# Transposes of the queries and of the pool layers' first mixed group one strip later, inverses behind the second queries, blocks for the solve collected by column: a four-layer decoder trunk on one core

## The chip, the core and the metric

The kernel runs on one core of a Trainium2 chip. The metric is the device time of one execution in microseconds (us), the median of several runs; less is better.

The core's engines work side by side, each through its own queue in order: TensorE (PE in the profile, with its weight loads as PEld) does the matmuls and transposes, VectorE (DVE), ScalarE (ACT) and GpSimd (POOL) the elementwise work, and SyncE (SP) issues the weight transfers. An instruction waits at the head of its queue until the semaphores it needs are set, and everything behind it on that engine waits too.

## What is computed

The reference is a trunk of four residual layers over 256 tokens of width 1024, and a final normalization:

```
for i in range(DEPTH):                       # 4
    kind, j = i % N_MIXERS, i // N_MIXERS    # 0 pool, 1 GDN, 2 MLA
    h = rmsnorm(x, norm_g[i])
    y = mixer[kind](h, ...)
    x = x + y
return rmsnorm(x, final_g)

def pool_mixer(h, w_in, w_grp, scale, w_out):
    u, gate = split(h @ w_in)                # 2 x 2048 columns
    p = windowed causal means of u, minus u  # 4 groups of 512 channels
    p = einsum('bsgi,gio->bsgo', p, w_grp)
    return (p * scale * silu(gate)) @ w_out

def gdn_mixer(h, w_in, conv_w, ...):         # 8 heads, chunks of tokens
    q, k, v, gate, b, a = split(h @ w_in)
    q, k, v = silu(causal_depthwise_conv(q, k, v))
    A = I + strict_lower(beta k k^T * decay)
    u, w = solve(A, [beta v, beta k exp(g)]) # triangular solve
    ...                                      # recurrence over the chunks
    return (rmsnorm(o) * silu(gate)) @ w_out
```

Layers 0 and 3 are pool layers, layer 1 is the GDN (gated delta rule) layer, layer 2 is MLA attention.

## The kernel before

**Strips.** All products with weights go through `project`, one strip of 512 weight columns at a time. SyncE loads 512 KB of weights; ScalarE rounds them (`whi`, a cast, L149 or L153), VectorE or, for a few, GpSimd takes the rest (`wlo`, L150 or L154); TensorE then multiplies three times for each product, at L162. In the channel form (`chan`) a strip has 96 matmuls of 128x256 and puts channels on the partitions. In the row form it has 48 matmuls of 128x512 and puts tokens on the partitions. Products go to banks of PSUM, transposes to others (`tp`), small matmuls to `aux`.

**Who sets the order.** A scheduler orders the instructions of every engine. `later(ins, ...)` binds what is written inside it behind the instructions named. The kernel keeps such marks in `mark`: `strip` is the last matmul of the last channel strip, `conv` the last step of the last convolution on VectorE, `dve` the last `wlo` there, `back` the last copy of the blocks on GpSimd.

**GDN layer.** Its steps stand in a list: `g` gate strips (row form), `k` and `q` strips of keys and queries in two halves, `v` values, `V` and `c` the last values in two parts, `d` decays, `a` the lower triangles, `s` the substitution, `b` the blocks back, `i` the inverses, `n` the query norms, `u` the first chunk's news. A half of keys or queries is one channel strip, a convolution over its four tiles (first tap on ScalarE at L768, three more on VectorE at L771), a silu on ScalarE (L813), and eight 128x128 transposes into `tp` (L819), whose squares are summed (L822, L823). `against` multiplies keys with queries or keys (L832). The solve: lower triangles LT (L841) are copied in blocks of 32x32 into Lg (ScalarE L864, GpSimd L866), transposed on VectorE (L869) and solved row by row on GpSimd (L875, L879). `blocks_back` transposes the result (L885) and copies it into T, two copies on ScalarE (L892) and two on GpSimd (L894). `inverses` transposes T on VectorE (L961) and joins the blocks with matmuls (L970, L976, L984, L988, L994).

**Pool layers.** For each group of 512 channels, in the order 3, 2, 1, 0, there is a gate strip, a strip of the inputs, the window sums, and one step behind it `mixed`, the product with the group's weights. The first group has the row form: its result y (L587) is turned by eight transposes (L593) before it can go into the output product. In `mixed` of that group they are written directly behind L587, between other strips.

**The head.** `Normed.rest` makes each layer's normalized input in pieces `h` (L399, L404) from two buffers, and `Final` writes them to the output with a transfer for each.

Of the kernel before, what the change touches and what calls it, by code (L numbers as in the profile page):

```python
# [42 lines left out]
def trunk(ctx: ExitStack, tc: tile.TileContext, x, positions, norm_g, pool_w_in, pool_w_grp,  # L43
# [130 lines left out]
    def project(src, ks, act, cols=CW, chan=False, tail=0, done=None, cuts=1,  # L174
# [29 lines left out]
        banks = [[bank(acc, "acc") for _ in range(cuts)] for _ in range(NT)]  # L204

        def rows(t, c, k0, n, parts):
            o, sl = banks[t][c][:, :width], slice(c * width, (c + 1) * width)
            for x, y in ((0, 0), (0, 1), (1, 0)) if n == 1 else ((0, None), (1, 0)):
                for j in range(n):
                    k = k0 + j  # L210
                    for z in (0, 1) if y is None else (y,):
                        mm(o, act(k, t * P, P)[x], parts[j][z][:, sl],
                           k == first and x == z == 0, k == last and x == 1, block or width)

        held = []
        for u, (k0, n) in enumerate(ks):
            held.append((k0, n, ready.pop(0) if ready else unit(k0, n)))
            if u < len(ks) - tail:
                now, held = held, []
            elif u == len(ks) - 1:  # L220
                now = held
            else:
                continue
            for t in range(NT):
                for c in range(cuts):
                    for one in now:
                        rows(t, c, *one)
                    if done and u == len(ks) - 1:
                        done(t, c, banks[t][c][:, :width])
        return [b[0] for b in banks]  # L230
# [146 lines left out]
    class Normed:  # L377
# [5 lines left out]

        def begin(self, t, a):
            sl = slice(a, a + CUT)
            self.early[t, a] = wh.tile([P, CUT], F32, tag="hg", name="hg")
            nc.gpsimd.tensor_tensor(out=self.early[t, a], in0=xs[t][:, sl], in1=self.g[:, sl],  # L387
                                    op=ALU.mult)

        def rest(self, t):  # L390
# [4 lines left out]
            for a in range(0, D, CW):  # L395
                h = wh.tile([P, CW], F32, tag="h", name="h")
                cut = CUT if (t, a) in self.early else 0
                sl = slice(a + cut, a + CW)
                nc.vector.scalar_tensor_tensor(out=h[:, cut:], in0=xs[t][:, sl], scalar=r[:, 0:1],  # L399
                                               in1=self.g[:, sl], op0=ALU.mult, op1=ALU.mult)  # L400
                hs.append(h)
                if not cut:
                    continue
                mark["rest"] = nc.scalar.activation(h[:, :CUT], self.early.pop((t, a)), AF.Copy,  # L404
                                                    scale=r[:, 0:1]).ins
# [29 lines left out]
    class Final(Normed):  # L435
        def __init__(self):
            super().__init__(final_g.rearrange("(a d) -> a d", a=1))

# [75 lines left out]
    def pool_layer(i, j, hT):  # L514
# [59 lines left out]
        def mixed(g, pT, gs):  # L574
# [13 lines left out]
            for a in range(2):  # L588
                ps = bank(tps, "tp")
                for b in range(2):  # L590
                    for t in range(NT):
                        c = 2 * a + b
                        nc.tensor.transpose(ps[:, b * S + t * P:b * S + (t + 1) * P],  # L593
                                            y[t][:, c * P:(c + 1) * P], ident)
                split_out((ps.rearrange("p (c s) -> p c s", c=2),
                           yT.many(g * 4 + 2 * a, 2, 0, S), None))

        waiting, loaded = None, []
        for g in order:
            gs = gate(g)  # L600
            if lead:
# [8 lines left out]
            if waiting:  # L610
                mixed(*waiting)
# [58 lines left out]
    def gdn_layer(i, j, hT):  # L670
# [23 lines left out]
        order = "g0 k0 d a0 k1 a1 s q0 g1 v0 v1 v2 b q1 i n V3 c3 g2 u0 u1 g3".split()  # L694
# [93 lines left out]
        Lg = LX[:, :M * B].rearrange("p (m c) -> p m c", m=M)  # L788
# [11 lines left out]
        def channels(dst, c0, hf, which):  # L800
# [4 lines left out]
            for b in range(2):  # L805
# [3 lines left out]
                for c in range(2):  # L809
# [3 lines left out]
                    mark["silu"] = nc.scalar.activation(o, v, AF.Silu).ins  # L813
            for c in range(0, 4, 2):
# [32 lines left out]
        def keys(hf):  # L847
            hs = slice(4 * hf, 4 * hf + 4)
            channels(kT, GDN_QK, hf, 0)
            n, r = ssq[:, 0, :, hs], s2[:, :, hs]  # L850
# [5 lines left out]
        def lower(hf):  # L856
            for t in range(NT):
                against(LT, kT, s2, hf, t)
                hs = slice(4 * hf, 4 * hf + 4)
                for d in range(Q):  # L860
                    dd = slice(d * B, (d + 1) * B)
                    o = Lg[dd, t * H + 4 * hf:t * H + 4 * hf + 4]
                    if t:
                        nc.scalar.copy(o, LT[t][dd, hs, dd])  # L864
                    else:
                        nc.gpsimd.tensor_copy(o, LT[t][dd, hs, dd])  # L866

        def substitution():
            nc.vector.transpose(Lb, Lg.rearrange("p m c -> p c m")[:, :, None, :].to_broadcast(  # L869
                [P, B, 2, M]))  # L870
# [12 lines left out]
        def blocks_back():  # L883
# [4 lines left out]
            for d in range(Q):  # L888
                dd = slice(d * B, (d + 1) * B)
                o = Ts[dd, :, :, dd].rearrange("p t h c -> p (t h) c")  # L890
                if d % 2:
                    nc.scalar.copy(o, tv[dd])  # L892
                else:
                    mark["back"] = nc.gpsimd.tensor_copy(o, tv[dd]).ins  # L894
# [3 lines left out]
        def queries(hf):  # L898
            if hf == 0:
                at_.extend(big("attnT", H, P) for _ in range(NT))  # L900
            channels(qT, 0, hf, 1)
# [101 lines left out]
        def news(hf):  # L1003
# [3 lines left out]
            for b in range(2):  # L1007
# [6 lines left out]
                for c in range(2):  # L1014
# [5 lines left out]
                 "c": values_done}  # L1020
        once = {"s": substitution, "d": decays, "b": blocks_back, "i": inverses,
                "n": query_norms}
        for name in order:
            if name in "bi":

                with later(mark["strip"], mark["dve" if name == "i" else "conv"]):
                    once[name]()
            elif name in once:
# [418 lines left out]
```

## Time and profile before

| | |
|---|---|
| runs | 809.26, 811.97, 812.18 us; median 811.97 |
| the profiled execution | 814.1 us, of it 812.4 us from first to last instruction |
| mean granted clock of TensorE | 0.994 |
| strips v0 to g3 of the GDN layer | about 230 to 320 us of the span |
| last pool layer's first mixed group | about 700 to 712 us |

Busy time is the time in which an engine executes. A window lists it for a stretch of the span, with the clock that TensorE was granted (1.00 is full speed). A timeline row is: start, length, engine, line, operation, result and operands, shapes, count, and in brackets the idle time just before it and what ended it. A row of the waits says who waited for whom: us in total, times, longest. Matmuls overlap, so that a row's length is longer than the distance to the next.

### The profile page before, as it was taken

The numbers are of one execution on the slowest core, as the hardware profiler recorded it, in microseconds if no ns is written. First come the engines' busy times: TensorE is split into PE (matmuls) and PEld (weight loads), VectorE is DVE, ScalarE is ACT, GpSimd is POOL, SyncE is SP. The second block draws the span as 40 slices with busy tenths as digits, with TensorE's granted clock in tenths as the row PEclk, the third lists the DMA queues.
The fourth block names the chain that finished last, engine by engine and source line by source line (L and its number), as shares of the span: only waits on it lengthen the run. The fifth ranks groups of instructions, "written<-read, shape, count | busy, mean of one in ns | idle before, by whom it ended". The sixth has DMA issues, their size and how long they took to land.

```text
span 812.4 us, 16075 instructions
## 1 busy us (share of the span) xinstructions
PE 795.3 (98%) x5966; PEld 754.5 (93%) x5966; DVE 601.3 (74%) x1134; ACT 498.6 (61%) x1007; POOL 132.7 (16%) x276
## 2 busy tenths in 40 slices
PE   8999999999989999999999999999999999999996
PEld 7989999989989988888989999999999989999996
DVE  4799898567999885466677659778777667877872
ACT  6666566568777745455566655566655575566662
POOL 3000000233238822022302003000000210000011
PEclk9999999999999989999999999999999999999999
DMA  6765656656555543223557676753542556575562
GB/s 208 228 196 170 198 204 225 216 156 209 181 154 167 174 130 115 94 79 109 179 182 231 194 182 189 201 148 86 181 157 79 182 161 189 194 224 196 193 220 53
DMA packets 106616, 138.85 MB, mean 171 GB/s; under 512 B 19045, under 2 KB 48937, under 8 KB 106537
## 3 DMA queue, kind: packets, MB, share of 16 engines
q1 hardware_dynamic: 104032, 136.07, 54.3%
q0 software_dynamic: 320, 1.06, 0.4%
q8 instruction: 47, 0.77, 0.4%
q10 hardware_dynamic: 2184, 0.69, 0.4%
q14 instruction: 33, 0.26, 0.1%
HBM read 136.74 MB, written 1.06 MB: 170 GB/s over the span
## 4 chain that ended last, share of the span: by engine, by line
PE 72%; DMA 8%; DVE 7%; POOL 5%; issue 4%; ACT 3%; ACTq 0%; SPq 0%; DVEq 0%
PE acc L162 57%; PE aux L162 7%; DMA raw<-in_pool_w_in_dram 3%; POOL U L879 2%; POOL X L875 2%; DMA raw<-in_gdn_w_in_dram 2%; DVE wlo L150 2%; DVE wlo L154 1%; DVE win L560 1%; ACT whi L153 1%; DMA Gb<-d_g 1%; ACT whi L149 1%; PE tp L1351 1%; DMA raw<-in_pool_w_out_dram 1%; DMA x<-in_x_dram 1%
## 5 line engine op out<-in xcount | busy, mean ns | idle before, releaser
L150 DVE TENSOR_TENSOR wlo<-raw,whi 128x512 fp32r<-128x512 f32 (+1 forms) x370 | 252.0, 707 | 100.7 <-ACT whi L149 98.6
L149 ACT CAST whi<-raw 128x512 fp32r<-128x512 f32 (+1 forms) x380 | 223.8, 617 | 153.5 <-PE acc L162 76.5
L162 PE MATMUL acc<-hTl,whi 128*128 128x256 f32 x832 | 231.4, 278 | 0.0
L162 PE MATMUL acc<-hTh,whi 128*128 128x256 f32 x832 | 229.9, 277 | 0.0
L162 PE MATMUL acc<-hTh,wlo 128*128 128x256 f32 x832 | 229.9, 277 | 0.0
L162 PEld LDWEIGHTS acc<-hTl,whi 128*128 128x128 f32 x832 | 160.6, 193 | 0.2
L162 PEld LDWEIGHTS acc<-hTh,whi 128*128 128x128 f32 x832 | 160.4, 193 | 0.3
L162 PEld LDWEIGHTS acc<-hTh,wlo 128*128 128x128 f32 x832 | 160.5, 193 | 0.1
L162 PE MATMUL acc<-wlo,yTh 128*128 128x256 f32 (+1 forms) x384 | 112.2, 311 | 0.7 <-DVE wlo L154 0.7
L162 PE MATMUL acc<-whi,yTh 128*128 128x256 f32 (+1 forms) x384 | 112.0, 315 | 0.0
L162 PE MATMUL acc<-whi,yTl 128*128 128x256 f32 (+1 forms) x384 | 89.0, 313 | 0.0
L162 PEld LDWEIGHTS acc<-wlo,yTh 128*128 128x128 f32 x384 | 73.2, 191 | 4.5 <-DVE wlo L154 1.5
L162 PEld LDWEIGHTS acc<-whi,yTh 128*128 128x128 f32 x384 | 72.9, 191 | 3.1
L162 PEld LDWEIGHTS acc<-whi,yTl 128*128 128x128 f32 x384 | 63.0, 191 | 3.3
L153 ACT ACTIVATE whi<-raw,colsT 128x512 fp32r<-128x512 f32 x64 | 44.0, 719 | 30.6 <-DMA raw<-in_pool_w_out_dram 15.9
L153 ACT ACTIVATE whi<-raw,gain 128x512 fp32r<-128x512 f32 x64 | 43.5, 719 | 29.1 <-DMA raw<-in_pool_w_in_dram 21.6
L154 DVE SCALAR_TENSOR_TENSOR wlo<-raw,colsT,whi 128x512 fp32r<-128x512 f32 x64 | 47.4, 767 | 18.6 <-ACT whi L153 18.1
L154 DVE SCALAR_TENSOR_TENSOR wlo<-raw,gain,whi 128x512 fp32r<-128x512 f32 x64 | 46.2, 744 | 13.0 <-ACT whi L153 11.3
L162 PE MATMUL acc<-wlo,hTh 128*128 128x512 f32 (+1 forms) x144 | 54.4, 383 | 0.4
L387 POOL TENSOR_TENSOR hg<-x,gain 128x256 f32<-128x256 f32 x16 | 13.3, 844 | 250.1 <-DVE x L451 202.0
L162 PE MATMUL acc<-whi,hTh 128*128 128x512 f32 (+1 forms) x144 | 53.1, 381 | 0.7 <-ACT hTh L242 0.7
L162 PE MATMUL acc<-whi,hTl 128*128 128x512 f32 (+1 forms) x144 | 42.5, 373 | 0.0
(367 smaller groups left out, 1505.1 us busy)
## 6 DMA issues: line engine op xcount, KB each, us to landing
raw<-in_pool_w_in_dram SPq DMA_DIRECT2D x62, 512.0 KB, 4.5
raw<-in_gdn_w_in_dram SPq DMA_DIRECT2D x48, 512.0 KB, 4.0
raw<-in_pool_w_out_dram SPq DMA_DIRECT2D x32, 512.0 KB, 4.5
raw<-in_mla_w_in_dram SPq DMA_DIRECT2D x24, 512.0 KB, 4.3
raw<-in_mla_w_uq_dram SPq DMA_DIRECT2D x36, 256.0 KB, 3.8
raw<-in_pool_w_grp_dram SPq DMA_DIRECT2D x16, 512.0 KB, 3.8
raw<-in_gdn_w_out_dram SPq DMA_DIRECT2D x16, 512.0 KB, 3.5
raw<-in_mla_w_ukv_dram SPq DMA_DIRECT2D x32, 256.0 KB, 3.4
```

The lines of the kernel that those rows point to most:

```text
L149: a = nc.scalar.copy(hi, v)
L150: b = e.tensor_tensor(out=lo, in0=v, in1=hi.bitcast(F32), op=ALU.subtract)
L153: a = nc.scalar.activation(hi, v, AF.Copy, scale=g)
L154: b = e.scalar_tensor_tensor(out=lo, in0=v, scalar=g, in1=hi.bitcast(F32), op0=ALU.mult, op1=ALU.subtract)
L162: return nc.tensor.matmul(inorder(o, n), lhsT=lhs, rhs=woven(rhs, n), start=start, stop=stop)
L387: nc.gpsimd.tensor_tensor(out=self.early[t, a], in0=xs[t][:, sl], in1=self.g[:, sl], op=ALU.mult)
L560: nc.vector.tensor_tensor(out=nxt[:, :, a:], in0=cur[:, :, a:], in1=cur[:, :, a - d:-d], op=ALU.add)
L875: nc.gpsimd.tensor_tensor(out=pv, op=ALU.mult, in0=Lb[:, r + 1:, r:r + 1].to_broadcast([P, n, c]), in1=Tb[:, r:r + 1, :c].to_broadcast([P, ...
L879: mark["blocks"] = nc.gpsimd.tensor_tensor(out=tv, in0=tv, in1=pv, op=ALU.subtract).ins
L1351: nc.tensor.transpose(ps[:, a * P:(a + 1) * P], sb[:, a * P:(a + 1) * P], ident)
```

## The change

Seven edits are made.

1. `project` in row form sets a new mark, `rows`, on its last matmul.
2. `Final` takes its pieces of h from another pool (`row`, four buffers) than the layers.
3. In the pool layers `mixed` of the first group returns its transposes as a closure, `turned`, which is called after the next gate strip and bound behind that strip's last matmul.
4. In the GDN layer `channels` is cut in two. Its transposes with their squares and sums are now `tokens`. Keys call both as before. Queries (`q`) call the first alone, and a new step `Q` does the rest: the transposes, `against`, and a product with the decays, bound behind the strip that stands ahead of it in the list. `Q0` stands after g1, `Q1` after V3. The query norms `n` go from behind `i` to behind g2.
5. The inverses are bound behind `conv`, the convolution of the second queries, instead of `dve`.
6. Lg is laid out by column and then by block instead of by block and then by column. The copies from LT are strided for that, and the transpose of Lg reads in order.
7. All four copies of `blocks_back` run on GpSimd.

```diff
@@ project
+        rows_end = [None]
...
-                        mm(o, act(k, t * P, P)[x], parts[j][z][:, sl],
-                           k == first and x == z == 0, k == last and x == 1, block or width)
+                        m = mm(o, act(k, t * P, P)[x], parts[j][z][:, sl],
+                               k == first and x == z == 0, k == last and x == 1, block or width)
+            rows_end[0] = m.ins
...
+        mark["rows"] = rows_end[0]
@@ Normed, Final
+        def piece(self):
+            return wh.tile([P, CW], F32, tag="h", name="h")
...
-                h = wh.tile([P, CW], F32, tag="h", name="h")
+                h = self.piece()
...
+        def piece(self):
+            return worka("row", CW)
@@ pool_layer
-        waiting, loaded = None, []
+        waiting, loaded, turned = None, [], None
         for g in order:
             gs = gate(g)
+            if turned:
+                with later(mark["strip"]):
+                    turned()
...
-            if waiting:
-                mixed(*waiting)
+            turned = mixed(*waiting) if waiting else None
@@ gdn_layer
-        order = "g0 k0 d a0 k1 a1 s q0 g1 v0 v1 v2 b q1 i n V3 c3 g2 u0 u1 g3".split()
+        order = "g0 k0 d a0 k1 a1 s q0 g1 Q0 v0 v1 v2 b q1 i V3 Q1 c3 g2 n u0 u1 g3".split()
...
-        Lg = LX[:, :M * B].rearrange("p (m c) -> p m c", m=M)
+        Lg = LX[:, :M * B].rearrange("p (c m) -> p c m", m=M)
...
-                    o = Lg[dd, t * H + 4 * hf:t * H + 4 * hf + 4]
+                    o = Lg[dd, :, t * H + 4 * hf:t * H + 4 * hf + 4]
+                    v = LT[t][dd, hs, dd].rearrange("p h c -> p c h")
                     if t:
-                        nc.scalar.copy(o, LT[t][dd, hs, dd])
+                        nc.scalar.copy(o, v)
                     else:
-                        nc.gpsimd.tensor_copy(o, LT[t][dd, hs, dd])
+                        nc.gpsimd.tensor_copy(o, v)
...
-            nc.vector.transpose(Lb, Lg.rearrange("p m c -> p c m")[:, :, None, :].to_broadcast(
-                [P, B, 2, M]))
+            nc.vector.transpose(Lb, Lg[:, :, None, :].to_broadcast([P, B, 2, M]))
...
-                if d % 2:
-                    nc.scalar.copy(o, tv[dd])
-                else:
-                    mark["back"] = nc.gpsimd.tensor_copy(o, tv[dd]).ins
+                mark["back"] = nc.gpsimd.tensor_copy(o, tv[dd]).ins
...
         def queries(hf):
+            channels(qT, 0, hf, 1)
+
+        def queries_done(hf):
             if hf == 0:
                 at_.extend(big("attnT", H, P) for _ in range(NT))
-            channels(qT, 0, hf, 1)
+            tokens(qT, hf, 1)
...
+        behind = "strip"
         for name in order:
+            if name[0] in "gkqvV":
+                behind = "rows" if name[0] == "g" else "strip"
             if name in "bi":
-                with later(mark["strip"], mark["dve" if name == "i" else "conv"]):
+                with later(mark["strip"], mark["conv"]):
                     once[name]()
+            elif name[0] == "Q":
+                with later(mark[behind]):
+                    queries_done(int(name[1]))
```

What the scheduler makes of it differs from the list at some places. Lines after the change are numbered anew: L813 becomes L828, L819 L836, L832 L849, L864 and L866 L883 and L885, L869 L888, L885 L903, L892 and L894 L909, L961 L979, L970 L988, L976 L994, L593 L604.

TensorE's queue in the first gate strip behind the second keys (g1), with the transposes of the second keys into `tp`, before; the first row is the 28th matmul of the strip:

```order
L162 MATMUL acc<-wlo,hTh_2253 128x512
L819 MATMUL tp<-ident,kqT 128x128 x2
L162 MATMUL acc<-whi,hTl_2254 128x512 x2
L162 MATMUL acc<-whi,hTh_2253 128x512
L832 MATMUL aux<-kqT 128x128
L819 MATMUL tp<-ident,kqT 128x128 x6
L832 MATMUL aux<-kqT 128x128 x7
```

and now, from the last matmul of the keys' own strip on:

```order
L162 MATMUL acc<-hTh_2253,wlo 128x256
L162 MATMUL acc<-whi,hTh_2244 128x512
L162 MATMUL acc<-wlo,hTh_2244 128x512
L162 MATMUL acc<-whi,hTh_2244 128x512
L162 MATMUL acc<-wlo,hTh_2244 128x512
L162 MATMUL acc<-whi,hTl_2245 128x512 x2
L836 MATMUL tp<-ident,kqT 128x128 x2
```

The keys' first two transposes moved from behind the 28th matmul of the strip to behind the 6th, and the other six are spread over the strip.

TensorE's queue in strip V3 (its matmuls are 128x256) and at the start of g2 (128x512), with the transposes of the second queries (`tp<-ident,kqT`) and the first products of the inverses (`aux<-T,LT` and `aux<-U,X`), before:

```order
L162 MATMUL acc<-hTh_2253,whi 128x256
L819 MATMUL tp<-ident,kqT 128x128 x2
L832 MATMUL aux<-kqT 128x128 x2
L970 MATMUL aux<-T,LT 128x64 x8
L162 MATMUL acc<-hTl_2254,whi 128x256
```

and now, at the end of the strip:

```order
L162 MATMUL acc<-hTh_2253,wlo 128x256
L836 MATMUL tp<-ident,kqT 128x128 x3
L994 MATMUL aux<-U,X_2489 96x64 x8
L988 MATMUL aux<-T,LT 128x64 x8
L836 MATMUL tp<-ident,kqT 128x128 x5
L162 MATMUL acc<-whi,hTh_2244 128x512
```

The piece of before stands after 76 of the strip's 96 matmuls; the piece of now is behind the 96th. Eight other products with T (L988), which the piece doesn't show, stand after the 57th.

VectorE's queue at the convolution of the second queries (`cv<-acc,tap,cv`), before:

```order
L150 TENSOR_TENSOR wlo<-raw,whi 128x512
L771 SCALAR_TENSOR_TENSOR cv<-acc,tap,cv 128x254
L961 STREAM_TRANSPOSE U<-T 128x1024 x2
L771 SCALAR_TENSOR_TENSOR cv<-acc,tap,cv 128x255
L771 SCALAR_TENSOR_TENSOR cv<-acc,tap,cv 128x253
```

and now:

```order
L150 TENSOR_TENSOR wlo<-raw,whi 128x512
L786 SCALAR_TENSOR_TENSOR cv<-acc,tap,cv 128x254
L786 SCALAR_TENSOR_TENSOR cv<-acc,tap,cv 128x253
L979 STREAM_TRANSPOSE U<-T 128x1024 x2
L990 TENSOR_TENSOR X_2489<-aux,m_627 128x16x32
```

The two transposes moved from behind the second of the convolution's twelve steps to behind the last.

More of the change, by code (lines that the diff above doesn't have):

```diff
@@ L587, in mixed, with turned @@
                 nc.vector.tensor_tensor(out=o, in0=v, in1=halves(gs[t], CW), op=ALU.mult)
[L588 to L596, printed above, removed]
-        waiting, loaded = None, []
+            def turned():
+                for a in range(2):
+                    ps = bank(tps, "tp")
+                    for b in range(2):
+                        for t in range(NT):
+                            c = 2 * a + b
+                            nc.tensor.transpose(ps[:, b * S + t * P:b * S + (t + 1) * P],
+                                                y[t][:, c * P:(c + 1) * P], ident)
+                    split_out((ps.rearrange("p (c s) -> p c s", c=2),
+                               yT.many(g * 4 + 2 * a, 2, 0, S), None))
+            return turned
+        waiting, loaded, turned = None, [], None
         for g in order:
             gs = gate(g)
+            if turned:
+                with later(mark["strip"]):
+                    turned()
             if lead:
@@ L813, in channels, with tokens @@
                     mark["silu"] = nc.scalar.activation(o, v, AF.Silu).ins
+        def tokens(dst, hf, which):
             for c in range(0, 4, 2):
@@ L849, in keys @@
             channels(kT, GDN_QK, hf, 0)
+            tokens(kT, hf, 0)
             n, r = ssq[:, 0, :, hs], s2[:, :, hs]
@@ L1019, in gdn_layer @@
         steps = {"g": gate, "k": keys, "a": lower, "q": queries, "v": values, "u": news, "V": values_in,
-                 "c": values_done}
+                 "c": values_done, "Q": queries_done}
         once = {"s": substitution, "d": decays, "b": blocks_back, "i": inverses,
                 "n": query_norms}
+        behind = "strip"
         for name in order:
+            if name[0] in "gkqvV":
+                behind = "rows" if name[0] == "g" else "strip"
             if name in "bi":
-                with later(mark["strip"], mark["dve" if name == "i" else "conv"]):
+                with later(mark["strip"], mark["conv"]):
                     once[name]()
+            elif name[0] == "Q":
+                with later(mark[behind]):
+                    queries_done(int(name[1]))
             elif name in once:
```

## The prediction

> **What bounds the kernel now.** I read the page first, then the windows, then the waits of the windows in which TensorE is short of work, and last the timelines of the engines there. From the page, the busy time of each engine and the chain that ended last:
>
> ```profile
> PE 795.3 (98%) x5966; PEld 754.5 (93%) x5966; DVE 601.3 (74%) x1134; ACT 498.6 (61%) x1007; POOL 132.7 (16%) x276
> ...
> PE 72%; DMA 8%; DVE 7%; POOL 5%; issue 4%; ACT 3%; ACTq 0%; SPq 0%; DVEq 0%
> ```
>
> TensorE is busy 98% of the span, and the change neither adds nor removes one of its matmuls. So what it can win is TensorE's idle time and time at a low clock, and nothing else. Windows of 20 us (length, busy of PE, PEld, DVE, ACT, POOL, granted clock, DMA share, GB/s) show where these lie near the change:
>
> ```profile
> 240.00:260.00 20.00, 18.11 (x163) 18.03 (x163) 19.50 (x38) 14.69 (x30) 17.57 (x32) 1.00 0.61 173
> 280.00:300.00 20.00, 18.30 (x137) 18.11 (x137) 15.34 (x25) 11.37 (x22) 7.19 (x6) 0.83 0.41 127
> ...
> 700.00:720.00 20.00, 19.13 (x162) 18.68 (x161) 17.22 (x25) 12.33 (x22) 0.15 (x1) 1.00 0.55 174
> ```
>
> Two lie in the GDN layer and one in the last pool layer. TensorE's own rows in the first two (start, length, idle before):
>
> ```profile
> 239.80 0.28 PE L162 MATMUL acc<-hTh,whi 128*128 128x256 f32 x1
> 241.97 0.44 PE L819 MATMUL tp<-ident,kqT 128*128 128x128 f32 x2 [1.90 <-ACT kqT L813]
> ...
> 287.96 0.28 PE L162 MATMUL acc<-hTh,wlo 128*128 128x256 f32 x1
> 288.07 0.28 PE L162 MATMUL acc<-hTh,whi 128*128 128x256 f32 x1
> 290.04 0.44 PE L819 MATMUL tp<-ident,kqT 128*128 128x128 f32 x2 [1.70 <-ACT kqT L813]
> ```
>
> Matmuls start 0.11 us apart (287.96, 288.07), so the first hole costs 241.97 - 239.80 - 0.11 = 2.06 us and the second 290.04 - 288.07 - 0.11 = 1.86 us. Both wait for the same thing: the transposes of the queries (L819) stand among the matmuls of the next strip, and the silu that feeds them (L813) is late. After the second hole the granted clock falls:
>
> ```profile
> 288.00:290.00 2.00, 0.34 (x4) 0.15 (x2) 2.00 (x5) 1.06 (x3) 0.63 (x2) 1.00 0.06 24
> 290.00:292.00 2.00, 1.96 (x15) 1.96 (x15) 2.00 (x5) 0.50 (x1) 0.00 (x0) 0.81 0.29 35
> 292.00:294.00 2.00, 2.00 (x11) 2.00 (x11) 2.00 (x5) 0.00 (x0) 0.00 (x0) 0.50 0.92 281
> 294.00:296.00 2.00, 2.00 (x11) 2.00 (x11) 0.94 (x3) 1.39 (x4) 0.00 (x0) 0.50 1.04 393
> 296.00:298.00 2.00, 2.00 (x11) 2.00 (x10) 1.44 (x4) 0.85 (x2) 1.28 (x1) 0.50 0.25 90
> 298.00:300.00 2.00, 2.00 (x21) 2.00 (x21) 1.28 (x2) 0.60 (x1) 0.00 (x0) 0.98 0.42 108
> ```
>
> The loss is 2 x (0.19 + 0.5 + 0.5 + 0.5 + 0.02) = 3.42 us, more than the wait itself. The longer first hole left the clock at 1.00. [...] The small waits, from the waits in the windows 700 to 712 and 800 to 812.4 us:
>
> ```profile
> PE tp L593 <- DVE y L587: 0.9, 1, 0.9
> ...
> DVE h L399 <- DMA out_dram<-h: 0.4, 1, 0.4
> ACT h L404 <- DMA out_dram<-h: 0.3, 1, 0.3
> ```
>
> **First queries (Q0).** What makes the first hole: ScalarE runs in order, and its silu stood behind casts that waited for a weight transfer.
>
> ```profile
> 240.44 1.14 ACT L149 CAST whi<-raw 128x512 fp32r<-128x512 f32 x2 [1.46 <-DMA raw<-in_gdn_w_in_dram]
> 241.48 0.43 ACT L813 ACTIVATE kqT<-cv 128x256 f32<-128x256 f32 x1
> ```
>
> The change puts these transposes some 18 to 25 matmuls later in strip v0, 2.0 to 2.8 us at 0.11 each, for a hole of 2.06. The silus keep their place among the casts, and TensorE itself comes no earlier up to there, so most of the hole goes: I leave 0.3 us (0 to 1). Gain 2.06 - 0.3 = 1.8.
>
> **Second keys, a wait that the change brings.** With Q0 elsewhere the scheduler also sets the transposes of the second keys, which no edit names, 6 matmuls into strip g1 where they stood 28 into it. In the trace of before these places are:
>
> ```profile
> 215.53 0.38 PE L162 MATMUL acc<-whi,hTh 128*128 128x512 f32 x1
> ...
> 216.83 0.38 PE L162 MATMUL acc<-whi,hTh 128*128 128x512 f32 x1
> ...
> 221.58 0.39 PE L819 MATMUL tp<-ident,kqT 128*128 128x128 f32 x2
> ```
>
> and on ScalarE:
>
> ```profile
> 215.59 1.14 ACT L149 CAST whi<-raw 128x512 fp32r<-128x512 f32 x2 [1.64 <-PE acc L162]
> ...
> 219.77 1.28 ACT L813 ACT_TABLE_LOAD   x1
> 221.07 0.73 ACT L813 ACTIVATE kqT<-cv 128x256 f32<-128x256 f32 x2
> ```
>
> In the new order the table load and the first silu stand two casts earlier, behind the first of the pair at 215.59: 215.59 + 0.57 + 1.28 + 0.42 (half of the two-silu row, with its overlap) = 217.9, for a TensorE that is there at 216.83. That is a new wait of 1.1 us. If the first cast is early it is 0.6, and if the silu stayed where it is (done by 221.5) it would be 4.7. I take 0.9. What is queued behind it is the rest of strip g1. So the first region gains 1.8 - 0.9 = 0.9 us.
>
> **Second queries, inverses, blocks.** Three things made the second hole:
>
> ```profile
> 279.93 2.18 ACT L892 COPY T<-U 32x512 f32<-32x512 f32 x2 [1.77 <-DVE U L885]
> ...
> 282.66 0.83 ACT L768 ACTIVATE cv<-acc,tap 128x256 f32<-128x256 f32 x2
> ...
> 289.56 0.43 ACT L813 ACTIVATE kqT<-cv 128x256 f32<-128x256 f32 x1
> ```
>
> and on VectorE, in the middle of the queries' convolution:
>
> ```profile
> 286.36 2.35 DVE L961 STREAM_TRANSPOSE U<-T 128x1024 f32<-128x1024 f32 x2
> 288.64 1.21 DVE L771 SCALAR_TENSOR_TENSOR cv<-acc,tap,cv 128x255 f32<-128x255 f32 x3
> ```
>
> The change takes the copies off ScalarE (2.18 us ahead of the convolution's first step L768), puts the two transposes (2.35) behind the convolution, and puts the queries' transposes at the end of V3, 20 matmuls or 2.2 us later. Together these are 4.5 us or more of lead for a wait of 1.86, so it goes whole, and with it, I take, the halved clock: 1.86 + 3.42 = 5.3.
>
> What is late next is T. All four copies now run on GpSimd, one after another, and TensorE asks for T in the middle of V3 (L970, now L988, 57 matmuls in, where the first hole's matmul at 288.07 was the 76th). The prices:
>
> ```profile
> 278.82 1.07 DVE L885 STREAM_TRANSPOSE U<-U 128x512 f32<-128x512 f32 x1 [1.50 <-POOL U L879]
> ```
>
> and, of line L894 (least, median, longest ns),
>
> ```profile
> L894 POOL COPY T<-U x2: 1057/1244/1430, 280.0 to 281.5; 32x512 f32<-32x512 f32 x2
> ```
>
> T is whole at 278.82 + 1.07 + 4 x 1.06 to 1.43 = 284.1 to 285.6. TensorE comes to L988 at 288.07 - 19 x 0.11 = 286.0, less the 0.9 gained above, 285.1; were the whole 2.06 gained, 284.0. The wait is 0 to 1.6 us; I take 0.4. Behind the convolution the two transposes end 2.35 us later than their wish, and L976 (now L994) at V3's end needs them and one more VectorE step: 0 to 1 us, 0.3 taken. Region gain 5.3 - 0.7 = 4.6.
>
> **Columns of the blocks.** The copies LT to Lg read and write with a stride now (shape 32x32x4 for 32x128), the transpose of Lg without one:
>
> ```profile
> L864 ACT COPY X<-LT x8: 281/294/298, 223.3 to 233.3; 32x128 f32<-32x128 f32 x8
> ...
> L869 DVE STREAM_TRANSPOSE U<-X x1: 2036/2036/2036, 236.8 to 236.8; 128x1024 f32<-128x1024 f32 x1
> ...
> L961 DVE STREAM_TRANSPOSE U<-T x2: 1195/1211/1227, 286.4 to 287.5; 128x1024 f32<-128x1024 f32 x2
> ```
>
> The transpose should fall from 2.04 towards the 1.21 of the same size read in order: 0.8 us off VectorE, and off the head of the GpSimd chain that ends at T, which would bring T to 283.3 to 284.8. A strided ScalarE copy of 512 elements took 1.08 to 1.09 (the two of 2.18 above), so one of 128 costs between 1.08 / 4 = 0.27 and 1.08 for its 0.29 now. I take 0.4, nearer the row of its own size: 8 x 0.1 on ScalarE, which idles there. [...] I put 0 in the sum for the whole edit.
>
> **The rest.** In the last pool layer y's transposes go behind the whole gate strip, which is 96 matmuls long, against a wait of 0.9: gain 0.9. In layer 0 I count nothing for the same move. The head's pieces of h come from four buffers instead of two, so that the two waits on the output's transfer go; they run side by side: gain 0.3. The later query norms on GpSimd have until the end of g2: nothing.
>
> **Sum.** 0.9 + 4.6 + 0.9 + 0.3 = 6.7 us. The profiled execution took 814.1 (span 812.4); 814.1 - 6.7 = 807.4. The median of the runs is 811.97, 2.1 below the profiled one, with one run at 809.26; 811.97 - 6.7 = **805.3**. A difference within 0.5%, 4.1 us, is no change that a measurement can tell: faster is below 807.9, slower above 816.0.
>
> **Rivals.**
> A: the new waits eat it. The second keys' silu keeps more of its old place (2.5 us instead of 0.9), Q0 keeps 1 us, T 1.4. For it: TensorE reaches the keys' transposes 4.7 us earlier in the order, and ScalarE's casts waited for transfers at each of these places. Against: the two casts that move. Cost (1.6 + 0.7 + 1.0) = 3.3, time 808.6. Chance 0.18.
> B: the clock halves all the same, in this place or after the new hole at 217 us. For it: one hole of 2 us did it and a longer one did not, so which hole does is not its length alone. Against: no hole as long should be left. [...] 805.3 + 3.4 = 808.7. Chance 0.15.
> C, slower: the strided copies are slow. They stand in ScalarE's queue right ahead of the silus of the second keys and of Q0. If each costs the 1.08 of the strided 512-element copy, four cost 3.1 us more, at two places, and TensorE waits that much more at both; two holes above 3 us halve the clock twice: -6.7 + 6.2 + 6.8 = +6.3, 818.3. It decides from about 1 us a copy; at half that nothing is lost but 0.8 us a place. Against: 128 elements, not 512. Chance 0.08.
> D: the order moves and the waits only change their names (the transposes wait at their new place as long as before), 812. Against: the moves are longer than the holes. Chance 0.04.
>
> **The numbers.** The forecast has 0.55. Its own range is 803.3 (all of 2.06 + 1.86 + 3.42 + 0.9 + 0.4 = 8.6 gained) to 807.5. The range goes down to 802.5, 0.8 under that for the scatter of the runs, and up to 811.5, where A and B meet (805.3 + 3.3 + 3.4 = 812, less the little that they share). Outside are C, D and little else. Faster: 0.55 and a third of A and B, 0.11, so 0.66. Slower: C, 0.08. The same: 0.26.
>
> **What would show it.** Right: no idle time ahead of the queries' transposes (L836) above 0.5 us, a granted clock of 1.00 from 280 to 300 us, a wait of about 1 us for kqT at 217 us, one of under 1.5 for T at L988, and an L888 of 1.2 us. Wrong: a clock of 0.5 anywhere in 200 to 320, L883 above 1 us, or a wait of more than 2 us at 217.

## The result and the profile after

The changed kernel takes 805.78 us (median of 5 runs, 804.58 to 807.01), the kernel before in the same series 812.18 (809.26 to 813.61): a ratio of 0.9931, 95% interval 0.9909 to 0.9953, which is 3.8 to 7.4 us less. Forecast were 805.3 and 6.7 less. The profiled execution took 805.67 us, 803.9 of it span, against 814.1 and 812.4.

The busy times and the chain that ended last, from the page of the changed kernel:

```profile
PE 790.5 (98%) x5966; PEld 750.1 (93%) x5966; DVE 601.1 (75%) x1134; ACT 497.0 (62%) x1005; POOL 139.0 (17%) x278
PE 92%; DVE 3%; ACT 1%; issue 1%; DMA 1%; POOL 0%; ACTq 0%; POOLq 0%; DVEq 0%
```

TensorE had 72% of that chain and now has 92%, but that is no measure of the gain: a second trace of the kernel before has 86% there. Of the 8.5 us between the two spans, 5.8 lie in the GDN layer, 1.5 in layer 0 and 1.1 in the last layer (the stretches are those of the next section). The same three windows as in the prediction (length, busy of PE, PEld, DVE, ACT, POOL, clock, DMA share, GB/s):

```profile
240.00:260.00 20.00, 20.00 (x180) 19.82 (x179) 19.25 (x38) 14.23 (x29) 17.73 (x30) 1.00 0.62 182
280.00:300.00 20.00, 19.16 (x163) 18.29 (x162) 19.82 (x35) 9.29 (x19) 10.95 (x11) 1.00 0.41 130
700.00:720.00 20.00, 20.00 (x182) 20.00 (x181) 15.23 (x24) 13.41 (x24) 0.00 (x0) 1.00 0.73 226
```

Both holes ahead of the queries' transposes are gone and the clock stays at 1.00. Two new waits stand in their place, in TensorE's timeline:

```profile
214.84 0.59 PE L162 MATMUL acc<-whi,hTl 128*128 128x512 f32 x2
216.24 0.44 PE L836 MATMUL tp<-ident,kqT 128*128 128x128 f32 x2 [0.80 <-ACT kqT L828]
...
288.90 0.49 PE L836 MATMUL tp<-ident,kqT 128*128 128x128 f32 x3
290.23 1.57 PE L994 MATMUL aux<-U,X 128*96 128x64 f32 x16 [0.84 <-DVE X L990]
```

Taken from start to start, less the step that is usual between such rows, the first costs 0.97 us and the second 1.00. The first is the wait for the second keys that the prediction put at 0.9. Behind it, on ScalarE:

```profile
213.84 0.62 ACT L149 CAST whi<-raw 128x512 fp32r<-128x512 f32 x1 [1.39 <-DMA raw<-in_gdn_w_in_dram]
214.48 1.28 ACT L828 ACT_TABLE_LOAD   x1
215.77 0.42 ACT L828 ACTIVATE kqT<-cv 128x256 f32<-128x256 f32 x1
```

This is the chain that was forecast, a cast, the table load of 1.28 and one silu, and the cast stood 1.39 us for its transfer. The second new wait, for the products `aux<-U,X` that join the blocks in pairs (below: the pairs), was forecast with 0.3. T itself came in time: the four copies on GpSimd end at 276.24 + 5.60 = 281.84, and TensorE's first product with T started at 282.76.

```profile
276.24 5.60 POOL L909 COPY T<-U 32x512 f32<-32x512 f32 x4 [1.19 <-DVE U L903]
...
282.76 1.90 PE L988 MATMUL aux<-T,LT 128*128 128x64 f32 x16
```

The layout by column, from the instructions of its lines (least, median, most ns):

```profile
L883 ACT COPY X<-LT x8: 416/418/423, 218.3 to 232.8; 32x128 f32<-32x128 f32 x8
L885 POOL COPY X<-LT x8: 395/675/1502, 213.3 to 231.8; 32x128 f32<-32x128 f32 x8
L888 DVE STREAM_TRANSPOSE U<-X x1: 1232/1232/1232, 234.9 to 234.9; 128x1024 f32<-128x1024 f32 x1
```

A copy on ScalarE is 0.42 for 0.29 (0.4 was forecast), the transpose 1.23 for 2.04 (1.2).

### The profile page after: what moved, and what is told of

It is laid out like the page before. It is cut to its first block, busy times and chain, and to the rows that moved or that the text cites. A ratio compares the mean times of both kernels' runs of the same rounds, so it can differ in the third digit from the quotient of the medians.

```text
span 803.9 us, 16071 instructions
## 1 busy us (share of the span) xinstructions
PE 790.5 (98%) x5966; PEld 750.1 (93%) x5966; DVE 601.1 (75%) x1134; ACT 497.0 (62%) x1005; POOL 139.0 (17%) x278
## 4 chain that ended last, share of the span: by engine, by line
PE 92%; DVE 3%; ACT 1%; issue 1%; DMA 1%; POOL 0%; ACTq 0%; POOLq 0%; DVEq 0%
PE acc L162 74%; PE aux L162 8%; DVE wlo L150 1%; PE aux L849 1%; PE tp L1376 1%; DVE cv L786 1%; DMA x<-in_x_dram 1%; DMA raw<-in_pool_w_in_dram 1%; PE tp L425 0%; PE tp L1110 0%; PE aux L1006 0%; PE aux L1073 0%; PE tp L836 0%; PE aux L1081 0%; PE aux L1090 0%
## 5 line engine op out<-in xcount | busy, mean ns | idle before, releaser
L162 PE MATMUL acc<-wlo,yTh 128*128 128x256 f32 (+1 forms) x384 | 112.2, 311 | 0.7 <-DVE wlo L154 0.7
```

The lines of the kernel that those rows point to most:

```text
L162: return nc.tensor.matmul(inorder(o, n), lhsT=lhs, rhs=woven(rhs, n), start=start, stop=stop)
```

## The experiments

In every trace I took four stretches of TensorE's timeline: from its first matmul to the first of the GDN layer's first strip (layer 0), from there to the first of the MLA layer's first strip (the GDN layer), then MLA, then the last layer to its last matmul. MLA took 247.05 us in all traces. The last layer took 150.91 in all but the first trace of before (152.00). Layer 0 took 163.5 to 167.2, with no order between the kernels. Only the GDN layer tells them apart. The holes are those of TensorE over 0.25 us in this layer's strips, without one of 0.3 at its start that all traces have; the clock's loss is summed from windows of 2 us. Ratios are those of a kernel's runs to runs of the kernel before in the same series. They are not quotients of the medians: for the changed kernel that would be 805.78 / 812.18 = 0.9921.

| kernel | GDN layer us | holes us | clock's loss us | median us | ratio, 95% interval |
|---|---|---|---|---|---|
| before | 239.8 | 4.5 | 3.4 | 812.18 | |
| before again | 239.4 | 4.1 | 3.4 | 812.78 | 1.0011 (0.9995 to 1.0027) |
| before, edit 6 alone | 236.7 | 4.9 | 0 | 811.06 | 0.9986 (0.9969 to 1.0004) |
| before, edit 7 alone | 235.6 | 2.0 | 1.7 | 809.17 | 0.9961 (0.9944 to 0.9978) |
| after without edit 6 | 237.8 | 2.6 | 3.4 | 810.30 | 0.9979 (0.9952 to 1.0007) |
| after without edit 7 | 235.4 | 3.3 | 0 | 807.65 | 0.9949 (0.9927 to 0.9971) |
| after without edit 5 | 234.0 | 1.7 | 0 | 807.03 | 0.9931 (0.9917 to 0.9946) |
| after, Q1 at q1 | 233.9 | 1.6 | 0 | 807.78 | 0.9931 (0.9907 to 0.9955) |
| after, Q0, Q1 and n in place | 233.9 | 1.6 | 0 | 807.73 | 0.9938 (0.9920 to 0.9956) |
| after without edit 3 | 232.8 | 1.0 | 0 | 807.12 | 0.9958 (0.9935 to 0.9981) |
| after | 234.0 | 2.0 | 0 | 805.78 | 0.9931 (0.9909 to 0.9953) |
| after, table early | 233.4 | 1.6 | 0 | 807.59 | 0.9955 (0.9933 to 0.9977) |
| after, pairs later | 231.9 | 0 | 0 | 806.26 | 0.9934 (0.9909 to 0.9959) |
| after, both | 231.8 | 0 | 0 | 805.41 | 0.9925 (0.9901 to 0.9948) |

The columns add up: 231.8 without holes (the last row's own time), plus holes, plus the clock's loss gives the measured GDN time within 0.5 us in all fourteen rows (before: 231.8 + 4.5 + 3.4 = 239.7). So the theory that TensorE's holes, and the clock behind them, are what the time is made of holds in the traces. The rest scatters on top: the medians less the GDN time of the trace lie between 571.8 us (after, the lowest) and 574.4, and layer 0 alone varies by 3.7 us between the traces.

**Before once more.** No edit.

> The kernel before, profiled once more. Theory (holes of TensorE, and a clock that a hole halves): the hole ahead of the second queries' transposes is there again with 1.7 to 2.0 us, and the granted clock is 0.5 for some 7 us behind it; 812 us. [...]

The second hole was there again, longer, and the clock halved again, in TensorE's timeline and the windows:

```profile
287.17 0.28 PE L162 MATMUL acc<-hTh,whi 128*128 128x256 f32 x1
289.64 0.44 PE L819 MATMUL tp<-ident,kqT 128*128 128x128 f32 x2 [2.20 <-ACT kqT L813]
```

```profile
288.00:290.00 2.00, 0.35 (x3) 0.36 (x4) 2.00 (x6) 1.46 (x3) 0.23 (x1) 1.00 0.00 1
290.00:292.00 2.00, 2.00 (x12) 2.00 (x12) 2.00 (x6) 0.10 (x1) 0.00 (x0) 0.50 0.39 57
...
296.00:298.00 2.00, 2.00 (x17) 2.00 (x16) 1.41 (x3) 0.92 (x2) 1.28 (x1) 0.79 0.08 26
```

The holes were 1.70 (clock stays) and 2.36 us (clock halves). So the trace bears out the theory. The runs show that the halving doesn't come in every execution: over 74 executions of the kernel before in this study the mean granted clock was 0.995 or lower in 34, with a median of 813.2 us, and 0.998 or 0.999 in 25, with a median of 810.9. Of the changed kernel's 5 runs none was under 0.996. In the fourteen traces a mean of 0.995 or lower goes with a halved clock ahead of the last matmul, and one of 0.997 or more with none. By this sign, which is not the clock's timeline itself, the halving comes in about half of the executions of the kernel before and costs 2.3 us between these medians, or 2.1 against all the other 40. Of the 54 executions of the changed kernel and its variants, without the one that lacks edit 6, three had 0.995 or lower.

**The seventh edit alone**, all four copies on GpSimd:

```diff
-                if d % 2:
-                    nc.scalar.copy(o, tv[dd])
-                else:
-                    mark["back"] = nc.gpsimd.tensor_copy(o, tv[dd]).ins
+                mark["back"] = nc.gpsimd.tensor_copy(o, tv[dd]).ins
```

> The kernel before with the seventh edit alone: all four copies of the blocks on GpSimd. The order moves with it: the two transposes U<-T go behind the eleventh of the convolution's twelve steps, the second queries' transposes forward to 41 of V3's 96 matmuls. Theory (ScalarE and VectorE freed for the convolution take the second hole away, whatever the place of the queries' transposes): no single wait for kqT above 1 us there and no halved clock behind it, but TensorE waits up to 1.5 us for T, which GpSimd has whole at about 285.5 us: 808.5 to 810.5 us. Rival (the later place is needed): a hole of 1.5 to 3 us for kqT and the clock at 0.5 behind it, 812 to 814 us.

The second hole is gone without the later place: the only wait of TensorE for kqT above 0.25 us in the layer is the first queries' (waits from 230 to 300 us), and this time that one halved the clock.

```profile
PE tp L819 <- ACT kqT L813: 1.8, 1, 1.8
```

```profile
242.00:244.00 2.00, 2.00 (x12) 2.00 (x12) 2.00 (x4) 1.65 (x4) 1.76 (x4) 0.54 0.90 258
244.00:246.00 2.00, 2.00 (x13) 2.00 (x13) 1.44 (x3) 0.49 (x1) 1.76 (x4) 0.60 0.90 240
```

The median of 809.17 us lies in the theory's range, but the wait for T that belongs to it didn't come. This trace has a second halving, of 1.7 us, behind a hole of 1.96 us in layer 0. ScalarE is not all that changed with the copies. The scheduler also moved the two transposes of T on VectorE (`U<-T`) behind the eleventh of the convolution's twelve steps, where the kernel before has them behind the second:

```profile
288.11 0.86 DVE L771 SCALAR_TENSOR_TENSOR cv<-acc,tap,cv 128x253 f32<-128x253 f32 x2
288.89 2.35 DVE L958 STREAM_TRANSPOSE U<-T 128x1024 f32<-128x1024 f32 x2
291.18 0.43 DVE L771 SCALAR_TENSOR_TENSOR cv<-acc,tap,cv 128x253 f32<-128x253 f32 x1
```

**The sixth edit alone**, blocks by column:

```diff
-        Lg = LX[:, :M * B].rearrange("p (m c) -> p m c", m=M)
+        Lg = LX[:, :M * B].rearrange("p (c m) -> p c m", m=M)
...
-            nc.vector.transpose(Lb, Lg.rearrange("p m c -> p c m")[:, :, None, :].to_broadcast(
-                [P, B, 2, M]))
+            nc.vector.transpose(Lb, Lg[:, :, None, :].to_broadcast([P, B, 2, M]))
```

with the copies strided as in the change.

> The kernel before with the sixth edit alone: blocks for the solve by column. The transpose of Lg takes 1.23 us instead of 2.04. Theory (the edit only moves the chain of the solve on GpSimd, which ends 1 to 3 us earlier; the copies on ScalarE then clear the way of the convolution earlier, but the two transposes still stand in its middle): the second hole shrinks by as much as the chain moves, to 0 to 1 us, 809 to 811.5 us. Rival (the layout is worth its 0.8 us of VectorE and nothing of the hole): hole of 1.7 us or more and the halved clock again, 812 us.

The solve's result reaches VectorE 111.2 us after the layer's start instead of 112.2 and 112.6. The second hole of 1.9 to 2.4 us breaks into 0.97 and 1.45, and neither halves the clock. In the waits from 205 to 310 us all four are for the silu, and none is over 2 us:

```profile
PE tp L819 <- ACT kqT L813: 4.2, 4, 1.8
```

The theory's 0 to 1 us for the hole was too low, its time of 811.1 right. The layer is some 3 us shorter than before because the clock didn't halve; the holes are no shorter. The ratio doesn't exclude no change.

**The change without the seventh edit:**

> The changed kernel without the seventh edit: two of the four copies on ScalarE again. Theory (the edits against the second hole cover for each other; here the later place of the transposes does): T whole about 2.7 us earlier, the silus up to 2.2 us later, for the transposes at the end of V3 a wait of 0 to 1 us, and the wait of 1.0 for the inverses smaller: 805.3 to 806.8 us, no halved clock. Rival (the copies' move carries the gain): the second hole back with 1.5 us or more, 808 to 811 us.

No wait for the second queries and no halved clock. The theory puts that down to the later place of their transposes, and the trace doesn't show it: edits 5 and 6 are in this kernel too, and the two transposes of T stand behind the whole convolution although two copies are on ScalarE.

```profile
286.93 2.41 DVE L786 SCALAR_TENSOR_TENSOR cv<-acc,tap,cv 128x254 f32<-128x254 f32 x5
289.25 2.36 DVE L982 STREAM_TRANSPOSE U<-T 128x1024 f32<-128x1024 f32 x2
```

The first of the four silus ended at 284.6 us. At the old place, the 76th matmul of V3, TensorE was at 287.57, so by this trace the first would have been in time there as well. The layer is 1.4 us longer than the change's all the same, because the wait for the keys was 1.6 in this trace and the one for the pairs 1.3 instead of smaller. The time lies above the theory's range and short of the rival's.

**The change without the sixth edit:**

> The changed kernel without the sixth edit: Lg by block, copies in order. Theory (the layout moves the solve's chain by 0.8 us, and T had 0.9 us to spare at its first use): L888 takes 2.0 us, the copies 0.29 instead of 0.42 us, T is whole 0.8 us later or a little more, TensorE waits 0 to 0.5 us for it: 805.5 to 806.5 us. Rival (T is the next bound and the layout is what keeps it in time): a wait for T of 1 us or more, 807 us or more.

Both were wrong on T, and the rival was right on the time: 810.30. TensorE didn't wait for T. It waited 2.37 us for the pairs, and the clock halved (TensorE's timeline and a window):

```profile
294.37 1.57 PE L995 MATMUL aux<-U,X 128*96 128x64 f32 x16 [2.20 <-DVE X L991]
```

```profile
298.00:300.00 2.00, 2.00 (x10) 1.94 (x10) 1.00 (x2) 0.69 (x2) 0.00 (x0) 0.50 0.96 354
```

The cause is on VectorE:

```profile
279.26 1.07 DVE L904 STREAM_TRANSPOSE U<-U 128x512 f32<-128x512 f32 x1 [2.63 <-POOL U L898]
```

This transpose is at the head of VectorE's queue, waiting for the last step of GpSimd's solve, and the whole convolution of the second queries, the two transposes of T and the step that the pairs wait for stand behind it in order. From its start to the start of the pairs' products it is 15.1 us here (294.37 - 279.26), in the changed kernel (290.23 less the 275.08 of the row below), without edit 3 and with the table early, and 15.0 without edit 5. (Where an edit changes the order in between it is another length, 14.2 to 18.3 us in the other variants of the changed kernel.) What the solve is late, the pairs are late.

```profile
275.08 1.09 DVE L903 STREAM_TRANSPOSE U<-U 128x512 f32<-128x512 f32 x1 [1.15 <-POOL U L897]
```

Among the traces without a wait for the keys it starts 110.95 us after the layer's start here and 109.2 to 109.8 with the layout by column: 1.1 to 1.8 us, of which the transpose of Lg itself is 0.8. Of this kernel's 10 runs five had a clock of 0.992 to 0.994 and took 810.3 to 815.7; the five with 0.997 and more took 807.8 to 810.3.

**The change without the fifth edit**, the inverses bound behind `dve` again:

```diff
-                with later(mark["strip"], mark["conv"]):
+                with later(mark["strip"], mark["dve" if name == "i" else "conv"]):
```

> The changed kernel, but with the inverses bound behind the last wlo as before, not behind the convolution. Theory (the two transposes move at the scheduler's will, because T now comes late from GpSimd, and the binding does little): they stand one step of twelve earlier, the time stays within 0.5 us of the changed kernel's 805.8. Rival (the binding is what keeps them out of the convolution): the silus are 2.3 us later, the second queries' transposes wait 1 to 2 us, 807 to 811 us.

No wait for the second queries; the layer took what it took with the edit (234.0). The two transposes stand one step of twelve earlier in the order. The median is 1.2 us above the changed kernel's, outside the theory's 0.5 and at the lower end of the rival's, but with the same ratio to before; the wait that the rival's time rests on isn't there. With all copies on GpSimd the scheduler puts these transposes late by itself.

**The place of the queries' transposes.** Q1 back at q1, and all of Q0, Q1 and n back:

```diff
-... g1 Q0 v0 v1 v2 b q1 i V3 Q1 c3 g2 n u0 u1 g3
+... g1 Q0 v0 v1 v2 b q1 Q1 i V3 c3 g2 n u0 u1 g3
```

> The changed kernel, but with Q1 right behind q1, so that the second queries' transposes stand in the middle of V3 again, at 52 to 69 of its 96 matmuls; copies on GpSimd and the inverses behind the convolution stay. Theory (it is the later place that hides the silus): in the changed kernel the four silus end at 281.2, 284.1, 285.7 and 287.9 us and TensorE would ask for them from 282.3 on, so it waits 2 to 3 us in pieces, and the wait of 1.0 for the inverses goes: 806.8 to 807.8 us, and 3.4 more if the clock halves. Rival (the freed ScalarE and VectorE did it, and the place was not needed): no wait for kqT above 0.3 us, 805.0 to 806.0 us.

```diff
-... s q0 g1 Q0 v0 v1 v2 b q1 i V3 Q1 c3 g2 n u0 u1 g3
+... s q0 Q0 g1 v0 v1 v2 b q1 Q1 i n V3 c3 g2 u0 u1 g3
```

> The changed kernel, but with Q0 right behind q0, Q1 right behind q1 and n behind i: all edits but the later place of the queries' transposes. Theory: the second keys' transposes are back behind the 28th matmul of g1 (their wait of 1.0 us goes), the first queries' hole of about 2 us is back, and the second queries' transposes wait 2 to 4 us in pieces: 808 to 810 us, up to 813 with a halved clock. Rival (the place of the transposes is worth little, the rest of the change brought the gain): within 1 us of 805.8.

With Q1 back there is a wait of 0.85 us for the second queries instead of 2 to 3, and the pairs' 1.0 is gone: they cancel, and though the median lies in the theory's range, its trace gives no reason for it. With all back, the second hole stays away altogether, the keys' wait goes (their transposes are behind the 28th matmul again), and the first hole is back:

```profile
242.69 0.44 PE L836 MATMUL tp<-ident,kqT 128*128 128x128 f32 x2 [1.48 <-ACT kqT L828]
```

It is 1.64 us from start to start and left the clock at 1.00. So Q0's later place takes away 1.6 to 2.1 us and costs the keys up to 1.0; Q1's later place is worth nothing that these traces show once the copies are off ScalarE. On the time the first theory lost: 807.7 lies below its 808 to 810, and 1.9 above the changed kernel, outside the rival's 1.

**The change without the third edit:**

```diff
             turned = mixed(*waiting) if waiting else None
+            if turned:
+                turned()
+                turned = None
```

> The changed kernel without the third edit: the first mixed group's transposes where they stood in the pool layers. Theory: a wait of about 1.0 us for y in the last pool layer is back, and at most 0.3 us in layer 0: 806.8 us. Rival (the wait moves on to the next product anyway): no change, 805.8 us.

The last layer took 150.91 us, as with the edit, and so it did in before again and with edits 6 and 7 alone, which all have the old order there. The wait of 1.0 us for y was in one execution of five. Its median of 807.12 fits the theory, but its trace doesn't have the wait on which that rests, and nothing else in it is longer: its GDN layer of 232.8 lacks the keys' wait.

**The two new waits taken away.** The table of silu loaded early (a silu of one column behind the decays' exponentials), the second half of the pairs behind the second queries' transposes, and both:

```diff
                 for a in (*DT, Eb):
                     nc.scalar.activation(a, a, AF.Exp)
+                tiny = small("tiny", 1, bufs=1)
+                nc.scalar.activation(tiny, Eb[:, 0, :1], AF.Silu)
```

> The changed kernel with silu's table loaded right behind the decays' exponentials. Theory (it is the load of 1.28 us behind a cast that waited for its transfer that makes the second keys late): the first silu of the second keys ends about 1.3 us earlier, the wait of 1.0 us in g1 goes: 804.8 us. Rival (the transfer or the convolution is what it waits for): the wait stays above 0.6 us, 805.4 us or more.

```diff
-... g1 Q0 v0 v1 v2 b q1 i V3 Q1 c3 g2 n u0 u1 g3
+... g1 Q0 v0 v1 v2 b q1 i V3 Q1 j c3 g2 n u0 u1 g3
```

where `j` holds the products `aux<-U,X` of the pairs and all that follows of the inverses, bound behind the last transpose of Q1.

> The changed kernel with the second half of the inverses' pairs behind the second queries' transposes. Theory: the wait of 1.0 us for X at 288.9 us goes, nothing else is late: 804.8 us. Rival: the eight products of queries and keys that come forward with them wait for a bank or the pairs wait at their new place: 805.8 us or more.

> The changed kernel with both of its new waits taken away: silu's table is loaded right behind the decays' exponentials (by a silu of one column), and the second half of the inverses' pairs goes behind the second queries' transposes. Theory (each wait is worth its length): no wait for kqT in g1, none for X in front of the pairs, 1.0 + 1.0 us less than the changed kernel: 803.5 to 804.5 us. Rival (a wait that is taken away comes back a little later, behind the same VectorE queue or the same transfers): within 0.7 us of the changed kernel's 805.8.

The pairs' wait goes and doesn't come back: the GDN layer falls to 231.9 and 231.8 us. Whether the early table takes the keys' wait away can't be told, since it was missing from traces without that edit as well. It goes with the cast ahead of the table load: in the four traces with the keys' wait that cast had waited 1.37 to 1.45 us for its transfer, without edit 3 it was 0.38, without edit 6 it was 0.74 for TensorE, and with the pairs later alone it was 0.36:

```profile
215.30 0.63 ACT L149 CAST whi<-raw 128x512 fp32r<-128x512 f32 x1 [0.36 <-DMA raw<-in_gdn_w_in_dram]
215.94 1.28 ACT L828 ACT_TABLE_LOAD   x1
```

With both, no wait over 0.3 us is left on TensorE between the layer's start and the recurrence (a window of that kernel):

```profile
280.00:300.00 20.00, 20.00 (x174) 19.60 (x174) 19.93 (x35) 9.26 (x20) 12.01 (x11) 1.00 0.42 131
```

The runs don't show these 2.2 us, and by the medians all three kernels fall to the rival: 805.41 and a ratio of 0.9925 with both, against 805.78 and 0.9931, intervals almost the same. The kernel with both is the fastest by its median, but not shown to be faster than the changed one. One of the ten executions with the table early took 2103.27 us. It is in the median but not in the ratio, and nothing here says what happened in it.

## Why the prediction was right, step by step

All the signs that the prediction named for being right showed in the changed kernel's trace. Its steps held less evenly.

- **What bounds the kernel.** Right: TensorE's holes and the clock explain the GDN layer in all fourteen traces.
- **First queries.** Right in kind, a little low: the hole of 2.06 went whole, not 1.8; put back (Q0 in place) it is 1.64.
- **Second keys.** Right: 0.97 for 0.9, through the table load behind a waiting cast. That the size fits is in part luck, for the wait isn't there in every execution: 0.75 to 1.6 us in four traces with this order, under 0.3 in five others. The cast's wait for its transfer parts the two groups (1.37 and more, 0.38 and less); that it is the transfer which decides was not tried by itself.
- **Second hole.** Right that it goes, and right that there is more lead than needed. But the three leads are not three separate ones, and the traces point to VectorE. In the three traces in which the two transposes of T stand behind the second of the convolution's twelve steps (before twice, edit 6 alone) TensorE waits 1.86 to 2.42 us for the second queries. In the eleven in which they stand behind the eleventh or twelfth it waits about 1 us at most, whether two copies are on ScalarE (without edit 7) or the queries' transposes are at their old place in the list (edit 7 alone, queries in place). The 2.35 us of these transposes are about the length of the hole. No run moves them alone, so it isn't shown that the copies on ScalarE and the later place count for nothing. The binding of the inverses does nothing that shows beside edit 7, with which the scheduler moves them anyway; without edit 7 it may be what does it.
- **The clock.** Right for the executions in which it halves, mis-sized for the median: 3.42 was one execution's loss. By the mean clock it occurs in 34 of 74 and makes 2.3 us between the medians, so that as an estimate it is worth about 2.3 x 34 / 74 = 1.1 us on the whole, not 3.4.
- **T.** 0.4 us were put down, 0 came; T had 0.9 to spare. (The matmul at 288.07 from which that step counts is the one at the second hole, not at the first.)
- **The pairs.** Mis-sized: 0.3 put down, 1.00 measured. The prediction looked at the two transposes alone; what is late is VectorE's whole queue behind the head that waits for the solve.
- **Columns of the blocks.** The step that failed: "I put 0 in the sum for the whole edit". Its parts were priced right (0.42, 1.23), and TensorE doesn't wait for T without it either. But the end of the solve also sets when VectorE gets to the convolution and to the pairs. Without the edit the wait there is 2.37 instead of 1.00, the clock fell to 0.50 behind it, and the time is 810.30. Of the five edits undone one by one (3 to 7) it cost the most by the medians.
- **Last pool layer.** 0.9 was put down; on the median it is 0, since the wait was one execution's.
- **Head.** 0.3 put down, nothing shows: from the last matmul to the end it is 812.4 - 804.98 = 7.42 us before and 803.9 - 796.51 = 7.39 after. The two waits for the output's transfer are gone, and the pieces are ready 0.47 us earlier counted from the last matmul, but the end of the span isn't.

```profile
804.98 0.39 PE L162 MATMUL acc<-whi,yTl 128*128 128x256 f32 x2
...
807.99 0.48 DVE L399 SCALAR_TENSOR_TENSOR h<-x,xr,gain 128x256 f32<-128x256 f32 x1 [0.39 <-DMA out_dram<-h]
```

```profile
796.51 0.39 PE L162 MATMUL acc<-whi,yTl 128*128 128x256 f32 x2
...
798.65 0.88 DVE L405 SCALAR_TENSOR_TENSOR row<-x,xr,gain 128x256 f32<-128x256 f32 x2 [1.29 <-POOL xr L398]
```

- **The sum.** 6.7 for 6.4. The GDN layer's part was 5.5 (0.9 + 4.6), and the traces give 239.8 - 234.0 = 5.8 or, from the second trace of before, 5.4. The 1.2 us of the last layer and the head didn't come. In the medians of the runs the total agrees within the interval of 3.8 to 7.4, and that is in part luck. By the traces the holes of the GDN layer fall from 4.3 (the mean of the two) to 2.0; with 1.1 for the clock and a fifth of y's wait that is about 3.6 us as an estimate, a little under the interval. The rest lies outside these holes, perhaps in the scatter, and its cause stays open. How much each of the edits is worth in the median can't be read from medians that scatter so; the traces tell it for the GDN layer only.
- **Rivals.** A and B each came in part: the pairs' wait is one that eats the gain, and the halved clock came back where one edit was left out. C didn't come: the strided copy on ScalarE costs 0.42, not 1.08. GpSimd's, for which no run behind the forecast had shown a price, went from 0.28 to 0.40 at least, 1.4 times as long. The median went from 0.29 to 0.68, which is more than the stride: it is 0.41 with edit 6 alone and with the queries in place, and 0.29 in the new order without edit 6. What the new order adds to it is not shown.

## What to carry to other kernels

An instruction that waits at the head of an in-order queue charges its wait to everything behind it: the transpose at the head of VectorE's queue stood 1.15 us for the solve in the changed kernel and 2.63 without edit 6, and the pairs' products began 15.1 us behind its start in both. So ask what stands behind it and not only who uses its result. An edit can also work through the order that the scheduler makes of it: taking copies off one engine moved two transposes on another. So compare the orders before crediting the edit, and both make it alone and undo it alone. A wait, or a clock's fall, that one profile shows is a chance, not a constant (y's wait of 1.0 us came in one execution of five, a mean clock of 0.995 or lower in 34 of 74): look at a second execution before pricing it whole.

## What the runs showed of the hardware

The granted clock fell to half behind holes of TensorE of 1.86 us (before), 2.36 (before again) and 2.37 (without edit 6), for a loss of 3.4 us each, and of 1.95 and 1.96 us (both with edit 7 alone), for 1.7 each. Behind holes of 1.64 (queries in place), 1.70 (before again), 1.99 (edit 6 alone) and 2.06 us (before) it didn't. No hole of 1.7 us or less did it, and about 2 us is where these traces show it going either way.

The clock didn't fall at a fixed distance from the hole. In the trace of before it fell at 291.25 us, 1.21 behind the hole's end at 290.04. By the windows of 2 us it fell about 0.4 us behind the end in before again (289.64), 2.1 without edit 6 (294.37) and 0.3 behind the first queries' hole with edit 7 alone (241.85). It stayed low for 6.83 us in before, by the windows for about 6.8 in before again and without edit 6, and for about 3.4 with edit 7 alone.

The clock's own records show steps that don't start with the hole: in the trace of before the stretches between two changes of the clock are 279.89, 6.83 and 512.00 us long, which is 41, 1 and 75 times 6.827, and in the changed kernel's trace the one stretch is 791.89 us, 116 times that. That a hole lies inside one step doesn't decide by itself whether the clock falls: counted back from 291.25, each of the two holes of before does so (236.64 to 243.46 and 284.42 to 291.25), and the clock fell behind the second alone. What decides it is not shown.
